# Set-up of a hybrid GLA and attention step: the first modulation vectors in two halves of the features

## The chip, the cores and the metric

One core of one Trainium2 chip. The metric is device time of one execution in microseconds (us): the median of three runs. Engines are named TensorE (PE in the rows, PEld its weight loads), VectorE (DVE), ScalarE (ACT), GpSimd (POOL) and SyncE (SP, which issues most DMAs).

## What is computed

Two layers over 256 context and 1024 latent tokens of width 1024. Only the first step of the first layer matters here: both token groups are normalised and modulated by vectors from a conditioning vector, and the result is projected.

```python
mod_p = (jax.nn.silu(c_ctx) @ w_ada[l] + b_ada[l])[None, None, :]
mod_s = (jax.nn.silu(c) @ w_ada[l] + b_ada[l])[:, None, :]
sh_s, sc_s, gt_s = split_mod(mod_s)
hs = rms_norm(xs, norm_g[l]) * (1.0 + sc_s) + sh_s
...
proj = h @ w_in
q, k, v, gate = jnp.split(proj, [GLA_QD, 2 * GLA_QD, 2 * GLA_QD + GLA_VD], axis=-1)
...
z = ((h @ wa1[d]) @ wa2[d] + ba[d]).astype(jnp.float32)
```

`w_ada[0]` is 1024 x 3072; shift and scale of layer 0 are its first 2048 columns, 8 MB in f32.

## The kernel before, in words

The hidden state `h` lies transposed in SBUF as two f16 tensors, `hT_hi` and `hT_lo` (high and low part), 8 tiles of 128 features by 1280 tokens. Each weight is split in the same way into `whi` and `wlo`, after scaling by a power of two; a product is three f16 matmuls (high by high, low by high, high by low). `pow2` finds such a power: a maximum for each partition on VectorE, one TensorE matmul that brings it across partitions into bank `o`, and some five one-column VectorE instructions (L87 to L102). Tokens come in three groups and chunks: the first 512 latent ones (group and chunk 0), the second 512, the 256 context ones.

The set-up (in `emit`) goes in this order:
- SyncE issues loads of the four token tiles `x` of group 0 (512 KB each), of two weight stages `wst` (1 MB each: queries and keys of the first heads), and of `w_ada` in eight row blocks of 1 MB, 8 KB for each partition, which land in places that are empty so early: `whi` and `wlo` of weight tiles 1 and 2, then `hT_hi` and `hT_lo`. Small constants, the next stage and the tokens of groups 2 and 1 (`ys`) follow; the low-rank decay weights come by GpSimd's queue.
- `cond_vectors`: the conditioning rows are transposed, SiLU is formed, and `cst` holds it as matmul weights. `normalise`: squares on ScalarE, mean-square step `nt_r4a` (L118), power -1/2 on GpSimd, then the rows `x` are scaled on VectorE (L352). TensorE transposes them, VectorE copies them to `xT` (L1327).
- `fill` makes `whi` on ScalarE (L190) and `wlo` on VectorE (L191) for the two stages; `split_rank` does the same for the low-rank decay weights.
- `mod_rows` sums all 2048 modulation values in 32 matmuls in bank `A` (L268), four of 512 columns side by side; the sums are copied, transposed in bank `cs` (L277) and get their bias (`modT`).
- `affine` forms gain and shift and their common power of two; its maximum is `af_m`, whose inverse is `inv_h`. `modulate` makes `h` on ScalarE (L370), `hT_hi` on GpSimd or ScalarE and `hT_lo` on VectorE, eight tiles of features one after another.
- `qk_pair` multiplies chunk 0 with the queries and keys of head 0: 48 matmuls of 512 columns (L495) in two `mm` banks over the 8 feature tiles. `rank` (low-rank decay, chunk 0) follows, then `ys` is normalised, transposed and modulated, and `qk_pair` runs for chunk 1, and so on.

Instructions are put in order by a scheduler for each engine (`issue_after` names one that must stand ahead), and each engine works through its rows in that order.

## Time and profile before

| | us |
|---|---|
| median of 3 runs | 1306.46 |
| lowest, highest | 1306.09, 1312.27 |
| the profiled execution: its own time | 1307.08 |
| the profiled execution: span of the core | 1305.20 |
| mean granted TensorE clock | 0.984 |

The span is from the first to the last instruction of the profile. Times in the rows are counted from its start; the rows come from that one execution.

### The profile page before, as it was taken

The numbers are of one execution on the slowest core, as the hardware profiler recorded it, in microseconds if no ns is written. First come the engines' busy times: TensorE is split into PE (matmuls) and PEld (weight loads), VectorE is DVE, ScalarE is ACT, GpSimd is POOL, SyncE is SP. The second block draws the span as 40 slices with busy tenths as digits, with TensorE's granted clock in tenths as the row PEclk, the third lists the DMA queues.
The fourth block names the chain that finished last, engine by engine and source line by source line (L and its number), as shares of the span: only waits on it lengthen the run. The fifth ranks groups of instructions, "written<-read, shape, count | busy, mean of one in ns | idle before, by whom it ended". The sixth has DMA issues, their size and how long they took to land. (4 is left out here: it accounts for less than half of the span.)

```text
span 1305.2 us, 22423 instructions
## 1 busy us (share of the span) xinstructions
PE 1222.4 (94%) x8015; PEld 791.3 (61%) x8015; DVE 907.5 (70%) x2110; ACT 713.3 (55%) x1730; POOL 370.9 (28%) x625
## 2 busy tenths in 40 slices
PE   4899999999998998798999889999999999989998
PEld 2366666555655556566877466667666666766444
DVE  5585879777876798666664667777667577786652
ACT  3684656565655566542443566666766677673110
POOL 1132214323322244311332643342233344322000
PEclk8899999999999999899999999999999999999999
DMA  9602745554646344257643376666947747879342
GB/s 366 245 33 82 219 149 179 168 158 130 189 139 195 116 150 142 82 150 261 162 120 108 91 179 130 126 131 133 202 105 167 141 87 145 175 151 236 126 153 81
DMA packets 335792, 199.12 MB, mean 153 GB/s; under 512 B 229838, under 2 KB 320446, under 8 KB 333376
## 3 DMA queue, kind: packets, MB, share of 16 engines
q1 hardware_dynamic: 328512, 180.79, 52.9%
q0 software_dynamic: 3728, 11.55, 2.7%
q10 hardware_dynamic: 3440, 5.35, 1.1%
q8 instruction: 63, 1.03, 0.3%
q14 instruction: 49, 0.40, 0.1%
HBM read 104.31 MB, written 37.24 MB: 108 GB/s over the span
## 5 line engine op out<-in xcount | busy, mean ns | idle before, releaser
L129 PEld LDWEIGHTS <-hT_hi 128*128 128x128 f16 x1920 | 188.7, 98 | 126.3 <-issue 12.8
L129 PE MATMUL mm<-whi,hT_hi 128*128 128x512 f16 (+1 forms) x576 | 200.6, 349 | 5.5 <-ACT gx L526 4.8
L129 PE MATMUL mm<-whi,hT_lo 128*128 128x512 f16 (+1 forms) x576 | 200.7, 348 | 0.0
L129 PE MATMUL mm<-wlo,hT_hi 128*128 128x512 f16 (+1 forms) x576 | 200.7, 348 | 0.0
L1094 DVE SCALAR_TENSOR_TENSOR phl<-p,srec,phl 128x1280 f16<-128x1280 f32 (+1 forms) x80 | 108.0, 1355 | 74.3 <-POOL phl L1091 43.5
L129 PEld LDWEIGHTS <-whi 128*128 128x128 f16 x1232 | 120.5, 98 | 61.6 <-issue 3.1
L129 PE MATMUL mm<-hT_hi,whi 128*128 128x256 f16 (+1 forms) x480 | 141.3, 294 | 0.7 <-ACT rope L1014 0.7
L129 PE MATMUL mm<-hT_lo,whi 128*128 128x256 f16 (+1 forms) x480 | 141.3, 294 | 0.0
L129 PE MATMUL mm<-hT_hi,wlo 128*128 128x256 f16 (+1 forms) x480 | 141.2, 294 | 0.0
L1061 PE MATMUL S<-kT,wst 128*128 128x512 f16 (+1 forms) x624 | 124.7, 342 | 11.5 <-ACT p L1069 11.5
L129 PEld LDWEIGHTS <-hT_lo 128*128 128x128 f16 x960 | 94.5, 98 | 61.6 <-issue 1.4
L129 PE MATMUL mm<-PT,vh 128*128 128x256 f16 x672 | 113.8, 275 | 8.8 <-DMA PT<-phl 6.0
L1091 POOL TENSOR_SCALAR phl<-p,srec 128x1280 f16<-128x1280 f32 (+1 forms) x40 | 55.4, 1384 | 200.4 <-DVE srec L1085 74.2
L1064 DVE TENSOR_REDUCE smx<-S 128x1 f32<-128x1280 f32 (+1 forms) x80 | 101.5, 1268 | 11.7 <-PE S L1061 11.7
L1069 ACT ACTIVATE p<-S,snb,sexp 128x1280 f32<-128x1280 f32 (+1 forms) x80 | 99.3, 1242 | 8.6 <-DVE phl L1094 3.7
L1061 PEld LDWEIGHTS <-wst 128*128 128x128 f16 x624 | 61.6, 99 | 66.1 <-issue 15.6
L129 PE MATMUL mm<-PT,vl 128*128 128x256 f16 x336 | 92.3, 275 | 0.0
L152 DVE TENSOR_REDUCE wmx<-wst 128x1 f32<-128x512 f32 x104 | 64.7, 676 | 22.0 <-DMA wst<-in_gla_w_in 8.7
L129 PEld LDWEIGHTS <-wlo 128*128 128x128 f16 x616 | 60.3, 98 | 31.5 <-DVE wlo L1222 1.8
L129 PEld LDWEIGHTS <-vh 128*128 128x128 f16 x672 | 65.6, 99 | 19.9 <-issue 8.3
L1066 ACT ACTIVATE snb<-smx,nsexp 128x1 f32<-128x1 f32 x80 | 23.3, 291 | 85.0 <-DVE smx L1064 84.8
L901 POOL TENSOR_TENSOR rope<-hx,ropet 128x64 f32<-128x64 f32 x160 | 63.1, 424 | 18.8 <-ACT hx L1027 11.2
(358 smaller groups left out, 2724.2 us busy)
## 6 DMA issues: line engine op xcount, KB each, us to landing
wada<-in_w_ada SPq DMA_DIRECT2D x16, 1024.0 KB
wst<-in_gla_w_in SPq DMA_DIRECT2D x12, 1024.0 KB
wst<-in_att_w_in SPq DMA_DIRECT2D x10, 1024.0 KB
og_d<-gx SPq DMA_DIRECT2D x40, 128.0 KB
og_d<-og POOLq DMA_DIRECT2D x40, 128.0 KB, 2.8
wst<-og_d SPq DMA_DIRECT2D x5, 1024.0 KB
xr<-x_d SPq DMA_DIRECT2D x9, 512.0 KB
out<-xr ACTq DMA_DIRECT2D x17, 256.0 KB
```

The source lines that it names most:

```text
L129: self.nc.tensor.matmul(out, a, b, start=k == 0 and j == 0, stop=k == n - 1 and j == 2)
L152: nc.vector.tensor_reduce(mx[:, j : j + 1], st[:, 2 * j : 2 * j + 2, :], AX.XY, ALU.max, apply_absolute_value=True)
L901: nc.gpsimd.tensor_tensor(tv[:, h, :, w, :], xv[:, h, :, 1 - w, :], sn[:, :, w, :], ALU.mult)
L1061: nc.tensor.matmul(S[:, a : a + n], x, y, start=m == 0, stop=m == 2)
L1064: last = nc.vector.tensor_reduce(mx, S, AX.X, ALU.max).ins
L1066: nc.scalar.activation(nb, mx, AF.Copy, scale=self.nsexp)
L1069: nc.scalar.activation(p, S, AF.Exp, scale=self.sexp, bias=nb, accum_out=den)
L1091: nc.gpsimd.tensor_scalar(hi, p, r, 2.0 ** 14, ALU.mult, ALU.mult)
L1094: nc.vector.scalar_tensor_tensor(lo, p, r2, hi, ALU.mult, ALU.subtract)
```

## The change

The columns of `w_ada` are loaded in two halves: first shift and scale of features 0 to 511 in eight pieces of 0.5 MB (two runs of 2 KB for each partition), into `hT_hi` and `hT_lo`, then those of features 512 to 1023 into the weight tiles. `mod_half` sums each half in 16 matmuls, in bank `A` and then `kt`; odd and even row blocks go to separate parts and are added on VectorE. `affine_half` gives the first half a power of two from its own maximum; the second takes the larger of both. Feature tiles 0 to 3 are modulated by the first half, and `qk_pair` sums 24 matmuls over them; after the second half it sums the other 24 and adds (L546 of the changed kernel). `rescale` brings the first four feature tiles of chunk 0 to the common power, for `rank`. SiLU is formed ahead of the mean-square step, two of four rows are normalised and four of eight `xT` copies made on ScalarE, and `split_rank` stands ahead of the two fills.

```diff
@@ -243,43 +243,85 @@
     def cond_vectors(self, rows, brow):
         nc, cp = self.nc, self.const
+        self.cst = self.t(cp, [P, KT, 32], F32, "cst")
+        nc.vector.memset(self.cst, 0.0)
         ps = self.bank("z")
         nc.tensor.transpose(ps[:, 0:32], rows, self.ident[0:32, 0:32])
-        nc.tensor.transpose(ps[:, 32:80], brow, self.ident[0:48, 0:48])
         cT = self.t(cp, [P, 80], F32, "cT")
-        nc.vector.tensor_copy(cT, ps[:, 0:80])
+        nc.vector.tensor_copy(cT[:, 0:32], ps[:, 0:32])
         self.gT = cT[:, 16:32]
         self.bT = cT[:, 32:80]
-        c = self.t(cp, [P, 16], F32, "silu_c")
-        nc.vector.tensor_copy(c, cT[:, 0:16])
+        c = cT[:, 0:16]
         self.silu(c, 16, "ls16")
-        self.cst = self.t(cp, [P, KT, 32], F32, "cst")
-        nc.vector.memset(self.cst, 0.0)
-        nc.vector.tensor_copy(self.cst[:, :, 0:2], c.rearrange("p (i k) -> p k i", i=2))
+        last = nc.vector.tensor_copy(self.cst[:, :, 0:2], c.rearrange("p (i k) -> p k i", i=2))
+        ps = self.bank("cs")
+        nc.tensor.transpose(ps[:, 0:48], brow, self.ident[0:48, 0:48])
+        nc.vector.tensor_copy(self.bT, ps[:, 0:48])
         self.modT = [self.t(cp, [P, 16, 2], F32, f"modT{l}") for l in range(2)]
-    def mod_rows(self, rows):
-        nc = self.nc
-        ps = self.bank("A")
+        return last.ins
+    def mod_half(self, u, rows):
+        nc = self.nc
+        ps = self.bank(("A", "kt")[u])
         for k, r in enumerate(rows):
-            for j in range(4):
-                nc.tensor.matmul(
-                    ps[32 * j : 32 * j + 32, :], self.cst[:, k, :], r[:, 512 * j : 512 * j + 512],
-                    start=k == 0, stop=k == KT - 1, tile_position=(0, 32 * j), skip_group_check=True,
-                )
+            with ExitStack() as c:
+                if k >= KT // 2:
+                    c.enter_context(self.tc.issue_after(self.cross))
+                for v in range(2):
+                    j = 2 * (k % 2) + v
+                    nc.tensor.matmul(
+                        ps[32 * j : 32 * j + 32, :], self.cst[:, k, :], r[:, v, :],
+                        start=k < 2, stop=k >= KT - 2, tile_position=(0, 32 * j), skip_group_check=True,
+                    )
         m = self.t(self.p1, [P, 512], F32, "mod")
         nc.scalar.copy(m[:, 0:256], ps[:, 0:256])
         nc.vector.tensor_copy(m[:, 256:512], ps[:, 256:512])
         ps = self.bank("cs")
         for b in range(4):
             nc.tensor.transpose(ps[:, b * P : b * P + P], m[:, b * P : b * P + P], self.ident)
-        nc.vector.tensor_tensor(
-            self.modT[0].rearrange("p (j b) i -> p j b i", j=4),
-            ps.rearrange("p (b j r) -> p j b r", b=4, j=4)[:, :, :, 0:2],
-            self.bT[:, 0:16].rearrange("p (j b) -> p j b", j=4).unsqueeze(3).to_broadcast([P, 4, 4, 2]), ALU.add,
-        )
+        part = ps.rearrange("p (b q v r) -> p q v b r", b=4, q=2, v=2)[:, :, :, :, 0:2]
+        to = self.modT[0].rearrange("p (v u b) i -> p u v b i", v=2, u=2)[:, u]
+        bias = self.bT[:, 0:16].rearrange("p (v u b) -> p u v b", v=2, u=2)[:, u].unsqueeze(3)
+        nc.vector.tensor_tensor(to, part[:, 0], bias.to_broadcast([P, 2, 4, 2]), ALU.add)
+        nc.vector.tensor_tensor(to, part[:, 1], to, ALU.add)
+    def affine_half(self, u):
+        nc, sp = self.nc, self.const
+        f = slice(4 * u, 4 * u + 4)
+        sh, sc = (self.modT[0][:, 8 * v : 8 * v + 8, :] for v in range(2))
+        if u == 0:
+            self.g0 = self.t(sp, [P, KT, 2], F32, "g0")
+            self.af = self.t(sp, [P, 2], F32, "af")
+        g = self.g0
+        gT = self.gT[:, f].unsqueeze(2).to_broadcast([P, 4, 2])
+        nc.vector.scalar_tensor_tensor(g[:, f], sc[:, f], 1.0, gT, ALU.add, ALU.mult)
+        m = self.t(self.small, [P, 2], F32, "wmx")
+        for j, t in enumerate((sh, g)):
+            nc.vector.tensor_reduce(m[:, j : j + 1], t[:, f], AX.XY, ALU.max, apply_absolute_value=True)
+        a = self.af[:, u : u + 1]
+        nc.vector.scalar_tensor_tensor(a, m[:, 1:2], 32.0, m[:, 0:1], ALU.mult, ALU.add)
+        if u == 1:
+            nc.vector.tensor_tensor(a, a, self.af[:, 0:1], ALU.max)
+        s, inv = self.pow2(a)
+        n = 4 + 4 * u
+        self.gs, self.sh = (self.t(sp, [P, n, 2], F32, f"{t}{n}") for t in ("gs", "sh"))
+        nc.vector.tensor_scalar(self.sh, sh[:, 0:n], s, None, ALU.mult)
+        nc.vector.tensor_scalar(self.gs, g[:, 0:n], s, None, ALU.mult)
+        if u == 1:
+            self.ratio = self.mulcol(s, self.inv_h, sp, "ratio")
+        self.inv_h = self.t(sp, [P, 1], F32, f"invh0{u}")
+        nc.vector.tensor_copy(self.inv_h, inv)
+    def rescale(self, c):
+        a, n = CHUNKS[c]
+        for t in (self.hT_hi, self.hT_lo):
+            x = t[:, 0 : KT // 2, a : a + n]
+            self.nc.vector.tensor_scalar(x, x, self.ratio, None, ALU.mult)
     def ada_load(self, l, b, to):
         self.nc.sync.dma_start(to, self.I["w_ada"][l, :, b * 256 : b * 256 + 256].rearrange("(k p) n -> p k n", p=P))
@@ -341,7 +383,7 @@
         return g, sh, c
-    def normalise(self, xs, junk):
+    def normalise(self, xs, junk, act=False):
         nc = self.nc
         n = len(xs)
         ssq = self.t(self.sm, [P, n], F32, f"nt_s{n}")
@@ -349,7 +391,10 @@
             nc.scalar.activation(junk, x, AF.Square, accum_out=ssq[:, j : j + 1])
         r = self.rstd(ssq, D, f"nt_r{n}")
         for j, x in enumerate(xs):
-            last = nc.vector.tensor_scalar(x, x, r[:, j : j + 1], None, ALU.mult)
+            if act and j % 2:
+                nc.scalar.activation(x, x, AF.Copy, scale=r[:, j : j + 1])
+            else:
+                last = nc.vector.tensor_scalar(x, x, r[:, j : j + 1], None, ALU.mult)
         return last.ins
     def transpose(self, xs, k, tag):
@@ -483,18 +528,26 @@
         self.qk[h][which][c] = out
-    def qk_pair(self, h, c, wq):
+    def qk_pair(self, h, c, wq, ks=range(KT), add=False):
         a, n = CHUNKS[c]
         banks = [self.bank("mm") for _ in range(2)]
-        for k in range(KT):
+        for k in ks:
             hh, hl = self.hT(k, a, n)
             for which, ps in enumerate(banks):
                 o = 256 * which + 128 * (h % 2)
                 wh, wl = (t[:, k, o : o + P] for t in wq[0:2])
                 for j, (x, y) in enumerate(((wh, hh), (wl, hh), (wh, hl))):
-                    self.nc.tensor.matmul(ps[:, :n], x, y, start=k == 0 and j == 0, stop=k == KT - 1 and j == 2)
+                    self.nc.tensor.matmul(
+                        ps[:, :n], x, y, start=k == ks[0] and j == 0, stop=k == ks[-1] and j == 2
+                    )
         for which, ps in enumerate(banks):
-            self.qk_out(h, which, c, ps[:, :n])
+            if add:
+                out = self.qk[h][which][c]
+                self.nc.vector.scalar_tensor_tensor(
+                    out, ps[:, :n], self.inv_qk[h // 2][which], out, ALU.mult, ALU.add
+                )
+            else:
+                self.qk_out(h, which, c, ps[:, :n])
     def tok_proj(self, i, w, ps):
         hi, lo = w[0:2]
@@ -1312,42 +1365,57 @@
             xs = group(0)
             wq = k.wtile(0)
             qk = [k.load_qk(wq, 0, j) for j in range(2)]
-            to = []
-            for t in (*k.wtile(1)[0:2], *k.wtile(2)[0:2], k.hT_hi, k.hT_hi, k.hT_lo, k.hT_lo):
-                a = 4096 * (len(to) % 2) if len(to) > 3 else 0
-                t = t.rearrange("p k n -> p (k n)")[:, a : a + 4096].bitcast(F32)
-                load(t, I["w_ada"][0, len(to) * P : len(to) * P + P, 0 : 2 * D])
-                to.append(t)
+            places = [t.rearrange("p k n -> p (k n)")[:, 2 * D * j : 2 * D * j + 2 * D]
+                      for t in (k.hT_hi, k.hT_lo, *k.wtile(1)[0:2], *k.wtile(2)[0:2])
+                      for j in range(4 if t is k.hT_hi or t is k.hT_lo else 2)]
+            to = [[], []]
+            for u in range(2):
+                for kk in range(KT):
+                    t = places.pop(0).bitcast(F32).rearrange("p (v n) -> p v n", v=2)
+                    ap = I["w_ada"][0, kk * P : kk * P + P, 0 : 2 * D]
+                    load(t, ap.rearrange("p (v u n) -> p u v n", v=2, u=2)[:, u])
+                    to[u].append(t)
             w = k.gla_consts()
-            k.cond_vectors(rows, brow)
+            cst = k.cond_vectors(rows, brow)
             junk = k.t(k.p1, [P, D], F16, "junk")
-            last = k.normalise(xs, junk)
+            with tc.issue_after(cst):
+                last = k.normalise(xs, junk, True)
             xT = k.t(k.p1, [P, KT, 512], F32, "xT")
             for kk in range(KT):
-                nc.vector.tensor_copy(xT[:, kk, :], k.transpose(xs, kk, ("z", "mm")[kk % 2]))
+                ps = k.transpose(xs, kk, ("z", "mm")[kk % 2])
+                if kk % 2:
+                    nc.scalar.copy(xT[:, kk, :], ps)
+                else:
+                    nc.vector.tensor_copy(xT[:, kk, :], ps)
             with tc.issue_after(last):
+                k.split_rank(*w)
                 run(qk[0])
                 run(qk[1])
-                cross = k.cross
-                k.split_rank(*w)
+            k.mod_half(0, to[0])
+            k.affine_half(0)
+            for kk in range(KT // 2):
+                act, dve = k.modulate(xT[:, kk, :], kk, GROUPS[0][0], kk % 2 == 1)
+            k.fold_qk(0, wq)
+            k.qk_pair(0, 0, wq, range(KT // 2))
             k.gla_tables()
             ys = group(1)
             wv = k.wtile(1)
             vf = k.load_v(wv, 0)
-            with tc.issue_after(cross), tc.issue_after(k.cross):
-                k.mod_rows(to)
+            k.mod_half(1, to[1])
             late = [t.rearrange("p k n -> p (k n)").bitcast(F32) for t in k.wtile(2)[0:2]]
             zs = [late[0][:, D * j : D * j + D] for j in range(2)]
             for j, x in enumerate(zs):
                 load(x, xrow(I, GROUPS[2][0] + j))
-            k.gs, k.sh, k.inv_h = k.affine(0)
-            for kk in range(KT):
+            k.affine_half(1)
+            for kk in range(KT // 2, KT):
                 act, dve = k.modulate(xT[:, kk, :], kk, GROUPS[0][0], kk % 2 == 1)
             k.fold_qk(0, wq)
             with tc.issue_after(act.ins), tc.issue_after(dve.ins):
                 k.rank_scales()
                 k.normalise(ys, junk)
-            k.qk_pair(0, 0, wq)
+            k.qk_pair(0, 0, wq, range(KT // 2, KT), True)
+            with tc.issue_after(dve.ins):
+                k.rescale(0)
             nxt = k.rank(0)
             for kk in range(KT):
                 act, dve = k.modulate(k.transpose(ys, kk, banks[kk % 6]), kk, GROUPS[1][0], kk % 2 == 1)
```

TensorE, from the last w_ada sums to the first chunk's matmuls, before. `A` is the bank of the sums, `cs` their transposes, `af_m` the cross-partition maximum, `mm` the queries and keys.

```order
L268 MATMUL A_330<-hT_hi_71,cst_166 32x512 x8
L268 MATMUL A_330<-hT_lo_72,cst_166 32x512 x8
L277 MATMUL cs_366<-ident_79,mod_363 128x128 x4
L87 LDWEIGHTS af_m_382
L87 MATMUL o_384<-ident_79,af_m_382 128x128
L495 LDWEIGHTS whi_16_120
L495 MATMUL mm_465<-hT_hi_71,whi_16_120 128x512
```

The same place in the changed kernel: `A` takes the first half's sums, `kt` the second's, in pieces of four or two matmuls.

```order
L275 MATMUL A_322<-hT_lo_72,cst_160 32x512 x4
L275 MATMUL kt_440<-whi_20_126,cst_160 32x512 x2
L284 MATMUL cs_342<-ident_79,mod_339 128x128 x2
L275 MATMUL kt_440<-whi_20_126,cst_160 32x512 x2
L284 MATMUL cs_342<-ident_79,mod_339 128x128 x2
L275 MATMUL kt_440<-wlo_21_127,cst_160 32x512 x4
L87 LDWEIGHTS af_350
L87 MATMUL o_356<-ident_79,af_350 128x128
L275 MATMUL kt_440<-whi_22_128,cst_160 32x512 x4
L275 MATMUL kt_440<-wlo_23_129,cst_160 32x512 x2
L540 LDWEIGHTS whi_16_120
L540 MATMUL mm_394<-hT_hi_71,whi_16_120 128x512
```

Four pieces of the second half now stand ahead of the first half's cross-partition matmul, and seven ahead of its first `mm` matmul; the eighth stands behind the tenth of these.

TensorE in the changed kernel, where the first half of the queries and keys ends and the second begins:

```order
L540 MATMUL mm_395<-hT_lo_72,whi_16_120 128x512
L284 MATMUL cs_460<-ident_79,mod_457 128x128 x4
L87 LDWEIGHTS af_350
L87 MATMUL o_477<-ident_79,af_350 128x128
L540 LDWEIGHTS whi_16_120
L540 MATMUL mm_546<-hT_hi_71,whi_16_120 128x512
```

The transposes of the second half's sums stand behind the last matmul of the first half, and nothing but the cross-partition matmul stands between them and the second half's matmuls.

VectorE ahead of the cross-partition maximum, before: the last fill of the decay weights, then the sums.

```order
L422 SCALAR_TENSOR_TENSOR wa_25_139<-wada_149,p2s_301,wa_25_139 34x1024
L274 COPY mod_363<-A_330 128x256
L278 TENSOR_TENSOR modT_38_169<-cs_366,cT_155 128x32
L329 SCALAR_TENSOR_TENSOR gs_91_376<-modT_38_169,cT_155 128x16
L333 TENSOR_REDUCE wmx_379<-modT_38_169 128x1
L333 TENSOR_REDUCE wmx_379<-gs_91_376 128x1
L335 SCALAR_TENSOR_TENSOR af_m_382<-wmx_379 128x1
L92 TENSOR_REDUCE p2m_386<-o_384 128x1
```

The same place in the changed kernel (`af` is the first half's maximum):

```order
L281 COPY mod_339<-A_322 128x256
L100 TENSOR_SCALAR p2s_310<-p2e_308 128x1
L102 TENSOR_SCALAR p2i_312<-p2e_308 128x1
L288 TENSOR_TENSOR modT_38_177<-cs_342,cT_164 128x2x8
L289 TENSOR_TENSOR modT_38_177<-cs_342,modT_38_177 128x2x8
L191 SCALAR_TENSOR_TENSOR wlo_17_121<-wst_124,p2s_310,whi_16_120 128x2x256
L301 SCALAR_TENSOR_TENSOR g_82_349<-modT_38_177,cT_164 128x8
L304 TENSOR_REDUCE wmx_352<-modT_38_177 128x1
L191 SCALAR_TENSOR_TENSOR wlo_17_121<-wst_124,p2s_310,whi_16_120 128x2x256
L304 TENSOR_REDUCE wmx_352<-g_82_349 128x1
L191 SCALAR_TENSOR_TENSOR wlo_17_121<-wst_124,p2s_310,whi_16_120 128x2x256
L306 SCALAR_TENSOR_TENSOR af_350<-wmx_352 128x1
```

The fills of the second weight stage (`wst_124`) now stand between the steps of the maximum: seven of the eight fills ahead of `af`, the eighth between it and the reduction of its cross-partition matmul.

## Rows read from the trace of the kernel before

**Rows 1.** Busy time by stretch: us and (instructions) by engine, granted clock, DMA share, GB/s.
```profile
0.00:65.00 65.00, 41.10 (x218) 18.78 (x219) 37.39 (x99) 32.45 (x53) 8.58 (x17) 0.89 0.84 307
65.00:400.00 335.00, 324.02 (x2048) 200.09 (x2046) 257.86 (x681) 199.89 (x504) 95.96 (x164) 0.99 0.47 146
```

**Rows 2.** Timeline, second group: start, duration, engine, line, operation; idle before and its releaser.
```profile
50.91 1.05 ACT L349 ACTIVATE junk<-x 128x1024 f16<-128x1024 f32 x1
...
55.62 0.17 DVE L118 TENSOR_SCALAR nt_r4a<-nt_s 128x4 f32<-128x4 f32 x1 [2.30 <-ACT junk L349]
56.93 2.74 DVE L352 TENSOR_SCALAR x<-x,nt_r 128x1024 f32<-128x1024 f32 x4 [1.13 <-POOL nt_r L120]
...
57.12 0.38 PE L495 MATMUL mm<-hT_lo,whi 128*128 128x512 f16 x1
...
61.57 0.78 ACT L370 ACTIVATE h<-z,sh,gs 128x512 f32<-128x512 f32 x1 [0.43 <-PE z L358]
...
63.56 0.38 PE L495 MATMUL mm<-hT_hi,whi 128*128 128x512 f16 x1
```

**Rows 3.** Timeline, from the first group's mean square to the first projection.
```profile
12.15 0.17 DVE L118 TENSOR_SCALAR nt_r4a<-nt_s 128x4 f32<-128x4 f32 x1 [10.99 <-ACT junk L349]
...
13.55 2.74 DVE L352 TENSOR_SCALAR x<-x,nt_r 128x1024 f32<-128x1024 f32 x4 [1.23 <-DMA wst<-in_gla_w_in]
...
35.67 1.29 DVE L422 SCALAR_TENSOR_TENSOR wa<-wada,p2s,wa 34x1024 f16<-34x1024 f32 x1
...
39.55 0.90 PE L277 MATMUL cs<-ident,mod 128*128 128x128 f32 x4 [0.49 <-ACT mod L273]
...
41.12 0.16 DVE L335 SCALAR_TENSOR_TENSOR af_m<-wmx 128x1 f32<-128x1 f32 x1
...
42.90 2.22 ACT L370 ACTIVATE h<-xT,sh,gs 128x512 f32<-128x512 f32 x3 [3.40 <-DVE gs L338]
...
44.48 0.58 PE L495 MATMUL mm<-hT_hi,whi 128*128 128x512 f16 x1 [2.91 <-POOL hT_hi L374]
```

**Rows 4.** Timeline: DMA issues behind the w_ada loads, and TensorE's wait for the last.
```profile
19.53 0.34 SPq L401 DMA_DIRECT2D sum<-in_k_sum  x1
...
26.98 0.38 SPq L404 DMA_DIRECT2D onorm<-in_gla_onorm  x1
...
37.99 0.16 PEld L268 LDWEIGHTS A<-hT_lo,cst 128*32 128x32 f32 x8 [0.90 <-DMA hT_lo<-in_w_ada]
```

**Rows 5.** DMA packets of three stretches: 20 to 30, 39 to 45, 45 to 54 us.
```profile
DMA packets 578, 4.21 MB, mean 421 GB/s; under 512 B 64, under 2 KB 64, under 8 KB 64
...
DMA packets 942, 2.38 MB, mean 397 GB/s; under 512 B 64, under 2 KB 464, under 8 KB 941
...
DMA packets 2352, 3.22 MB, mean 358 GB/s; under 512 B 77, under 2 KB 2061, under 8 KB 2352
```

**Rows 6.** VectorE from 12 to 37 us by line: count, busy us, mean ns, idle.
```profile
L191 DVE SCALAR_TENSOR_TENSOR wlo<-wst,p2s,whi 128x512 f16<-128x512 f32 x8 | 5.6, 742 | 0.0
...
L1327 DVE COPY xT<-z 128x512 f32<-128x512 f32 x4 | 2.7, 687 | 0.2 <-PE z L358 0.2
L352 DVE TENSOR_SCALAR x<-x,nt_r 128x1024 f32<-128x1024 f32 x4 | 2.7, 748 | 1.2 <-DMA wst<-in_gla_w_in 1.2
L1327 DVE COPY xT<-mm 128x512 f32<-128x512 f32 x4 | 2.6, 680 | 0.0
```

**Rows 7.** Timeline: the first ScalarE and the first VectorE step of SiLU.
```profile
22.57 0.21 ACT L230 ACTIVATE ls<-silu_c 128x16 f32<-128x16 f32 x1 [10.45 <-DVE silu_c L254]
...
25.96 0.17 DVE L233 SCALAR_TENSOR_TENSOR ls<-silu_c,ls 128x16 f32<-128x16 f32 x1
```

**Rows 8.** Busy time by stretch around the first projection, columns as in rows 1.
```profile
42.00:44.00 2.00, 0.00 (x0) 0.00 (x0) 1.19 (x9) 1.10 (x2) 0.19 (x1) 0.69 1.03 412
44.40:49.50 5.10, 5.02 (x12) 1.72 (x12) 3.38 (x5) 5.07 (x9) 1.56 (x4) 0.50 1.04 391
49.50:57.20 7.70, 7.70 (x37) 3.44 (x35) 3.90 (x14) 6.27 (x12) 1.34 (x2) 1.00 0.63 201
```

## The prediction

> **What bounds the kernel now.** I read the busy time by stretch first [rows 1]: up to 65 us TensorE works 41.1 of 65 us, from 65 to 400 us 324 of 335. So after the set-up the kernel is a TensorE queue that hardly waits, and the order of every engine behind the first chunks is the same rows in both programs (the listings differ only up to the transposes of the second group). What the change is worth is therefore one number: how far the first matmul of the second chunk's queries and keys moves, at 63.56 us now [rows 2]. I let that shift reach the end unchanged, since TensorE's waits behind it are on other engines of the same chain.
>
> What holds that matmul now, read backwards in the timeline [rows 2, 3]: the w_ada rows land until TensorE's wait at 37.99 us ends [rows 4]; sum, transposes, maximum, cross-partition matmul and modulation take until the first matmul at 44.48 us; 48 matmuls run to 57.5 us. Beside them ScalarE modulates until 50.91 us, then takes the squares of the second group (to 55.6 us), VectorE scales those rows from 56.93 to 59.67 us, and transposes and modulation follow.
>
> **DMA.** Half of the w_ada bytes are there at about 27 us: each issue behind the eight loads waits for one landing, the one at 26.98 us for the fourth [rows 4]. Pieces become runs of 2 KB instead of 8 KB. Neither is in the trace; runs of 8 KB moved at 421 GB/s, of 4 KB (mostly) at 397, of 1 KB (mostly) at 358 [rows 5]. I take 387, between the last two: 1.35 us for each 0.52 MB piece, so from 17.0 us (27 less four megabyte loads of 2.5 us) the first half is there at 27.9, the fourth piece of the second half at 33.3, the seventh at 37.3 and the last at 38.7. At 358 the last is there at 40.4, at 421 at 37.0. The bytes are no longer the first thing waited for; the engines are.
>
> **VectorE in front of the first sum.** The order listing puts nearly all fills of the query and key weights ahead of the first half's maximum `af`. Before, VectorE worked from 13.55 us to 36.96 us (the row at 35.67 plus 1.29) [rows 3], 23.4 us with hardly a gap. Of this go: four `xT` copies to ScalarE (2.6), two of the four normalising rows (1.4) [rows 6], small copies and SiLU steps moved ahead (0.6) and one fill, now behind the maximum (0.7). New in front: the bank copy, two additions, the gain, two reductions and the maximum, 1.3 by the 0.16 to 0.42 us of such instructions, and 0.4 waiting for the transposes: 19.8 us. The start is later, because SiLU now stands ahead of the mean-square step of 12.15 us: four ScalarE and three VectorE steps of some 0.2 us each [rows 7], 1.7 us, so 15.2. `af` is at about 35.2, where it was 41.12. From `af` to the first matmul it was 3.36 us [rows 3]; 0.3 more for the last fill in between. The first half's matmuls start at **38.9 us instead of 44.48**. TensorE's order puts seven of the second half's eight pieces ahead of them, but these are done by about 37.8, just in time: that cover is 1 us.
>
> **First half.** 24 matmuls. Now, the engine stood from about 40.5 to 44.48 us but for one small matmul; the granted clock fell (0.69 over 42 to 44 us), was 0.50 (1.2 GHz) for the 5.1 us from 44.40 (12 matmuls, 0.43 us each) and full (2.4 GHz) after 49.50 (0.21 us) [rows 8]. In the new order TensorE is again in small pieces ahead of 38.9. I take the same price: 10 matmuls at 0.43, the last two w_ada matmuls of 0.5, the rest at 0.21: 7.9 us, to 46.8. At full clock it would be 5.6.
>
> **Between the halves.** This is what the new order adds: the transposes of the second half's sums stand behind the last of those 24 matmuls, and everything that follows needs them. The same chain, from transposes at 39.55 to matmul at 44.48, is 4.93 us now [rows 3]; one more addition and one more maximum add 0.3. TensorE has nothing else in its queue meanwhile. Second half: 46.8 + 5.2 = **52.0 us**. So the clock falls and is paid a second time: 12 matmuls at 0.43 and 12 at 0.21, 7.7 us, to **59.7 us instead of 57.5**. The Trainium skill, in TensorE: Matmul & The Clock Gate, section HAM oscillation — how this bites in real kernels, speaks against such a cut: matmul bursts with waits between them pay the slow clock for every burst instead of once, and all of the contraction should be done before the next wait. By that rule the price above is paid twice, as I sum it; before shows it for one burst only.
>
> **The second group.** ScalarE's first modulation comes 1.6 us ahead of the matmul [rows 3]; eight took 8.0 us (42.90 to 50.91), four take 4.0: squares from 52.0 - 1.6 + 4.0 = 54.4, not 50.91. They last 4.7 us, to 59.1. VectorE's next step in that chain stands behind the addition of the second half's queries: 59.7 + 0.2 + 0.7 = 60.6 (at 55.62 now). Then as now: 1.31 us to the scaling, 2.74 us for four rows, 64.6. Now TensorE is still busy when they are done (the first modulation follows at 61.57, 1.9 us behind the last row); in the new order TensorE waits for them, so 0.35 us, and 1.99 us from the modulation to the matmul: 67.0. The rescaling is two f16 instructions of 2048 elements, between 0.75 us (one f32 row of 1024) and 1.5 us each; it lies beside the second half's matmuls, and without that cover would delay `rank` by up to 3 us, of which the wait for the second group hides most. Loads of the second group stand earlier in the queue and are there by about 46 us, ahead of the squares.
>
> Sum: 67.0 - 63.56 = **+3.4 us**. On the profiled execution (span 1305.2, time 1307.08) it is 1310.5; that execution is 0.6 above the median of the runs, so 1306.46 + 3.4 = **1309.9 us**. 0.5%, about what a measurement of this kernel can tell from no change, is 6.5 us.
>
> **Rivals.**
> - *The clock is paid once or not at all.* For it: the w_ada matmuls run until 1 us before the first half. Against: the fall between 40.5 and 44.48 after just such a stretch. Full in the first half: 2.2 less at 46.8 and all behind, +1.2, 1307.7. Full in the second: squares then set the end, 1.4 less, +2.0, 1308.5. Full in both: -0.2, 1306.3.
> - *VectorE or the loads are later.* The new small instructions and the waits between ScalarE's and VectorE's fills may cost 2 us more, or loads at 358 GB/s hold the seventh piece to 39.0 us: +0.7 to +2, 1310.6 to 1311.9.
> - *Slower: TensorE never reaches the upper clock in either half.* With 0.43 us throughout, 24 matmuls and the two w_ada ones take 10.8 us (2.9 more) and the second 24 take 10.3 (2.6 more): +8.9, 1315.4. For it: each half is only a little longer than the 5.1 us that the low clock lasted. Against: it did rise after them. It decides from 15 further matmuls at 0.43 on; 3.1 us more than I sum is past 6.5.
> - *Faster, as one reads the diff: the first sums come with the bytes at 28 us.* `af` at about 30 us, the first half at 33.5 and done before the second's bytes end; the second half then starts some 5 us behind the last piece, at about 44.5 at the earliest, so 7.5 less than above and about -5 at the end, 1301.5; by over 0.5% only if the clock is full too. Against: 19.8 us of VectorE work stand in front in its order.
>
> **How the numbers follow.** Clock paid twice 0.45; once 0.23; not at all 0.12; later engines or loads 0.08; low clock throughout 0.08; first sums with the bytes 0.04. The first four lie within 1306.3 and 1311.9. With 1.8 us for the scatter of the runs and the uncertain VectorE sum below, and 1.1 above, the range is 1304.5 to 1313.0; it leaves out the last two cases. Faster by over 0.5% 0.04 (the last case), slower by over 0.5% 0.08 (the low clock throughout), within 0.5% 0.88.
>
> **What would show it.** Right: the first `mm` matmul near 39 us and the 25th near 52, TensorE idle some 5 us between with VectorE's small chain in it, granted clock 0.5 at the start of both, squares from 54 us, the second chunk's first matmul near 67, and the same spacing behind it. Wrong: `af` on VectorE near 30 (its sum is off), a full clock at either start, the last w_ada piece behind 44 us (2 KB runs are slow), or a shift at 65 us that is not there at the end.

## The result, and the profile after

The changed kernel took 1310.26 us (median of 20 runs, 1305.86 to 1320.71), the kernel before 1306.70 us beside it (20 runs, 1300.07 to 1312.27): 3.6 us more by the medians, a ratio of 1.0036 with an interval of 1.0023 to 1.0048 (4.7 us, 3.0 to 6.3, of 1306.7). That is inside the half per cent that the prediction called no change, and 0.4 us from its number. The steps under it came out less well, as the profile shows. For the set-ups run alone, below, medians are given over all runs and over those within 1.5% of the fastest run of the same kernel.

Busy time by stretch of the changed kernel, columns as in [rows 1]:

```profile
0.00:65.00 65.00, 40.28 (x217) 17.79 (x218) 38.90 (x116) 35.93 (x58) 8.33 (x16) 0.97 0.88 306
65.00:400.00 335.00, 324.09 (x2052) 200.00 (x2051) 258.62 (x683) 201.29 (x506) 95.16 (x164) 0.99 0.47 146
```

TensorE's share ahead of 65 us and behind it is that of before; the granted clock of the first stretch is 0.97 where it was 0.89.

The timeline of the set-up after (start, duration, engine, line, operation, idle time before and its releaser). It answers to [rows 2, 3]:

```profile
11.56 1.06 ACT L391 ACTIVATE junk<-x 128x1024 f16<-128x1024 f32 x1 [1.81 <-DMA x<-in_x_sample]
...
15.49 1.42 DVE L397 TENSOR_SCALAR x<-x,nt_r 128x1024 f32<-128x1024 f32 x2 [1.12 <-POOL nt_r L120]
...
36.28 0.15 DVE L306 SCALAR_TENSOR_TENSOR af<-wmx 128x1 f32<-128x1 f32 x1
...
38.34 1.05 PE L275 MATMUL kt<-wlo,cst 128*32 128x512 f32 x4 [0.31 <-DMA wlo<-in_w_ada]
...
39.88 0.38 PE L540 MATMUL mm<-hT_hi,whi 128*128 128x512 f16 x1 [0.48 <-POOL hT_hi L419]
...
46.14 0.60 PE L284 MATMUL cs<-ident,mod 128*128 128x128 f32 x4
...
48.00 0.23 PE L87 MATMUL o<-ident,af 128*128 128x128 bf16 x1 [1.26 <-DVE af L308]
...
51.14 0.58 PE L540 MATMUL mm<-hT_hi,whi 128*128 128x512 f16 x1 [2.90 <-POOL hT_hi L419]
...
57.83 0.75 DVE L546 SCALAR_TENSOR_TENSOR q<-mm,iqk,q 128x512 f32<-128x512 f32 x1 [0.63 <-PE mm L540]
...
58.49 0.16 DVE L118 TENSOR_SCALAR nt_r4a<-nt_s 128x4 f32<-128x4 f32 x1
...
64.94 0.38 PE L540 MATMUL mm<-hT_hi,whi 128*128 128x512 f16 x1
```

The first row is the square of the fourth token tile, which starts when that tile has landed. The first half starts at 39.88 us, behind a w_ada piece whose bytes held TensorE until 38.34. The transposes of the second half's sums (`cs`) come at 46.14, its first matmul at 51.14; the factors (`nt_r4a`) of the second group and the second chunk's first matmul (the last row) follow. That last row stood at 63.56 before [rows 2]: the set-up is 1.4 us longer in these two traces, not 3.4.

The clock, in the same columns, for the first half, the gap, and two pieces of the second half. It answers to [rows 8]:

```profile
39.80:46.10 6.30, 6.22 (x28) 2.45 (x28) 3.12 (x5) 2.93 (x6) 0.65 (x2) 1.00 0.95 339
46.10:51.10 5.00, 0.87 (x6) 0.47 (x5) 2.65 (x18) 2.79 (x5) 0.62 (x1) 0.97 1.07 355
51.10:54.20 3.10, 3.06 (x8) 1.11 (x8) 2.49 (x4) 3.07 (x5) 0.62 (x1) 0.50 1.09 354
54.20:57.80 3.60, 3.60 (x18) 1.49 (x16) 2.90 (x12) 3.50 (x7) 0.00 (x0) 0.99 0.74 283
```

The first half ran at 1.00 from its first matmul to its last. Only 8 matmuls of the second half ran in the stretch at 0.50.

SyncE's queue, which shows how fast the pieces land (each of these issues waited for a landing). It answers to [rows 4]:

```profile
19.34 1.77 SPq L1376 DMA_DIRECT2D whi<-in_w_ada  x2
...
30.19 0.48 SPq L446 DMA_DIRECT2D sum<-in_k_sum  x1
```

Eight issues lie between the two, 10.85 us: 1.36 us for a piece of 0.52 MB, 387 GB/s. The prediction took 1.35 us. Each piece landed about 1 us later than its sum has it: the seventh of the second half held TensorE until 38.34 us (37.3 in the prediction).

How the shift against the kernel before goes on behind the set-up, in us. I worked it out from the timelines of VectorE and ScalarE: the median, over all rows that stand in the same order in both kernels, of their start less their start before. The last three columns are experiments below.

```
stretch before   changed   again   overlap   8 steps   16 steps
  80 to  120       1.4      0.7     -1.0       3.6       3.6
 160 to  200       2.4      1.1     -0.8       4.9       3.6
 280 to  320       0.5     -0.2     -1.3       2.8       1.5
 360 to  400       0.4     -0.1      0.9       3.0       1.7
 400 to  440       0.9      0.3      1.2      -0.3       2.5
 680 to  720       1.1      0.7      1.5       2.3       1.8
 960 to 1000       1.7     -2.5      2.0       3.0      -0.8
1040 to 1080       3.9     -0.3      4.6       5.3       1.9
     end           5.9      1.1      5.0       8.6       3.7
```

Each column is one execution. Within a column the shift wanders by 4 to 9 us, with no stretch at which all lose, so one trace cannot place the few us behind the set-up; the medians must be asked. The executions differ as a whole too: that of the changed kernel took 1312.86 us, above its median, that of again 1308.05, below its own.

### The profile page after: what moved, and what is told of

Same layout as the page of the kernel before. It is cut to its first block, busy times and chain, and to the rows that moved or that the text cites. A ratio compares the mean times of both kernels' runs of the same rounds, so it can differ in the third digit from the quotient of the medians.

```text
span 1311.1 us, 22470 instructions
## 1 busy us (share of the span) xinstructions
PE 1227.1 (94%) x8020; PEld 791.8 (60%) x8020; DVE 910.7 (69%) x2128; ACT 718.8 (55%) x1737; POOL 371.3 (28%) x625
## 5 line engine op out<-in xcount | busy, mean ns | idle before, releaser
L1114 PE MATMUL S<-kT,wst 128*128 128x512 f16 (+1 forms) x624 | 126.0, 345 | 10.5 <-ACT p L1122 10.4
L954 POOL TENSOR_TENSOR rope<-hx,ropet 128x64 f32<-128x64 f32 x160 | 63.1, 425 | 19.8 <-ACT hx L1080 12.1
```

The costliest lines, as they stand in the source:

```text
L954: nc.gpsimd.tensor_tensor(tv[:, h, :, w, :], xv[:, h, :, 1 - w, :], sn[:, :, w, :], ALU.mult)
L1114: nc.tensor.matmul(S[:, a : a + n], x, y, start=m == 0, stop=m == 2)
```

## The experiments

My theory: the set-up sets the price, by the chain between the halves and the low clock, and what it loses arrives whole at the end. The rivals: the start of the first half sets it (VectorE or loads); the low clock alone sets it; what costs lies behind the set-up.

### The changed kernel again (again), and both set-ups alone (setup_before, setup_after, setup_before2)

The first is the changed kernel unaltered. The set-ups alone are both kernels cut off behind the second chunk's rank sums, with four query and key tiles stored and everything behind left out:

```diff
+            for which in range(2):
+                for c in range(2):
+                    o = O[1][0].rearrange("(a p) d -> a p d", p=P)[4 * which + 2 * c]
+                    load(o[:, 0:512], k.qk[0][which][c])
+            return
```

Expected of the first: 

> The changed kernel once more, unaltered, for a second profile. Theory A (the difference is made in the set-up, and what follows carries it): the second chunk's first matmul again near 64.9 us, 1.4 later than in the kernel before, and behind it a shift against the kernel before that wanders by some 2 us either way, not always to the later side. Theory B (the rest of the 3.6 us is made behind the set-up, always at the same places): the shift grows again to some 4 us by 1040 us and to 5.9 at the end. Time 1308 to 1312 by both.

Of the set-up before: 

> The kernel before, ended behind the set-up: it stops when the second chunk's queries, keys and decay rank are summed and stores four query and key tiles, everything later is left out. Both theories: the second chunk's first matmul at 63.6 us as in the whole kernel, a time near 90 us with a scatter well under 1 us. It is the base for the next run.

Of the changed set-up: 

> The changed kernel, ended at the same place, everything later left out. Theory A1 (the set-up makes 1.4 us, as in the profile, in every run): 1.2 to 1.6 us longer than the run of the kernel before that ends there. Theory A2 (in most runs the clock of the first half is low, as I had forecast, and the profile shows a lucky one): 3 to 4 us longer, with more scatter. Theory B as A1; the rest of the 3.6 us would then lie behind the set-up.

Of the set-up before a second time, on the chip of the last cuts: 

> The kernel before cut off behind the set-up once more (everything behind is left out), beside the other cuts on one chip: 85.1 us if the side edits' 0.8 us is theirs; 85.6 to 86.0 if it is the chip's.

Measured: again 1312.39 us (12 runs) beside 1307.78, ratio 1.0020 (1.0001 to 1.0039). The set-ups alone: 85.14 us before (84.49 to 86.41, a wider scatter than expected), 86.01 the second time (85.42 to 87.08), and 87.59 changed (85.48 to 88.45; five of eight runs at 87.5 to 88.5, three at 85.5 to 86.1). All set-ups that ran alone, with those below:

| set-up alone | chip | median of all runs, us | of those within 1.5% |
|---|---|---|---|
| before | 4 | 85.14 | 84.97 |
| before, second time | 7 | 86.01 | 85.75 |
| changed | 4 | 87.59 | 86.04 |
| setup_overlap | 0 | 85.09 | 85.09 |
| setup_warm | 0 | 87.00 | 86.80 |
| setup_silu | 0 | 86.98 | 86.52 |
| setup_side | 0 | 85.95 | 85.95 |
| setup_overlap1 | 7 | 84.64 | 84.63 |

So the changed set-up costs 1.6 to 2.5 us by the medians of all runs, and 0.3 to 1.1 us by the last column. One and the same set-up differs by 0.9 us between two chips, and the changed one was not run on the chip of the next four: differences of under 1 us between them show nothing, and the traces must tell the rest. What hangs least on the start of the loads is the time from the first half's first matmul to the second chunk's first: 25.06 us in the changed kernel.

The changed set-up alone, timeline of one of its five long runs:

```profile
12.33 1.06 ACT L391 ACTIVATE junk<-x 128x1024 f16<-128x1024 f32 x1 [1.78 <-DMA x<-in_x_sample]
...
16.26 1.42 DVE L397 TENSOR_SCALAR x<-x,nt_r 128x1024 f32<-128x1024 f32 x2 [1.12 <-POOL nt_r L120]
...
40.86 0.38 PE L540 MATMUL mm<-hT_hi,whi 128*128 128x512 f16 x1 [1.08 <-POOL hT_hi L419]
...
47.13 0.60 PE L284 MATMUL cs<-ident,mod 128*128 128x128 f32 x4
...
52.12 0.59 PE L540 MATMUL mm<-hT_hi,whi 128*128 128x512 f16 x1 [2.90 <-POOL hT_hi L419]
...
59.07 0.19 ACT L391 ACTIVATION_READ_ACCUMULATOR junk<-x 128x1 f32 x1
...
59.62 0.75 DVE L546 SCALAR_TENSOR_TENSOR q<-mm,iqk,q 128x512 f32<-128x512 f32 x1 [1.44 <-PE mm L540]
60.29 0.16 DVE L118 TENSOR_SCALAR nt_r4a<-nt_s 128x4 f32<-128x4 f32 x1
...
66.77 0.38 PE L540 MATMUL mm<-hT_hi,whi 128*128 128x512 f16 x1
```

and its second half by stretch, columns as above:

```profile
52.10:56.90 4.80, 4.78 (x12) 1.75 (x12) 4.20 (x10) 4.73 (x8) 0.62 (x1) 0.50 0.00 0
56.90:59.60 2.70, 2.70 (x14) 1.09 (x12) 1.19 (x7) 2.30 (x4) 0.00 (x0) 1.00 0.00 0
```

Two things differ from the profile of the whole kernel. The fourth token tile landed at 12.33 and not 11.56 us, and VectorE's scaling stands 3.93 us behind it in both (15.49 less 11.56, 16.26 less 12.33). From there to the first half it is mostly VectorE's work, so a late load arrives at the first matmul, 0.98 us there. And the low clock lasted for 12 matmuls and not 8, so the second half's queries are added (`q`) only at 59.62 and the factors behind them start at 60.29, 1.0 us behind the end of the squares (59.26); from the first matmul to the second chunk it is 25.91 us. That these two make the long runs is in part argued, as no short run of this set-up has a trace; the mean granted clock fits it (0.945 to 0.950 in the five long runs, 0.961 to 0.970 in the three short ones). In again it is 25.07 us:

```profile
39.23 0.38 PE L540 MATMUL mm<-hT_hi,whi 128*128 128x512 f16 x1
...
50.48 0.59 PE L540 MATMUL mm<-hT_hi,whi 128*128 128x512 f16 x1 [2.90 <-POOL hT_hi L419]
...
64.30 0.38 PE L540 MATMUL mm<-hT_hi,whi 128*128 128x512 f16 x1
```

The set-up before waits for the last bytes of w_ada instead, and its runs lie closer.

### Half of the first half behind the cross-partition step (setup_overlap)

```diff
-            k.qk_pair(0, 0, wq, range(KT // 2))
+            held = k.qk_pair(0, 0, wq, range(KT // 2), part=range(SPLIT))
...
             k.affine_half(1)
+            with tc.issue_after(k.cross):
+                k.qk_pair(0, 0, wq, range(KT // 2), part=range(SPLIT, KT // 2), banks=held)
...
```

(`qk_pair` gets the two arguments `part` and `banks`.)

Expected, with SPLIT = 2: 

> The changed kernel cut off behind the set-up (it ends once the rank sums of the second chunk are issued and stores four query and key tiles; everything behind is left out), with the last 12 of the first half's 24 matmuls put behind the second half's cross-partition matmul, so that the bias transposes of the second half and its cross-partition matmul come 12 matmuls (12 x 0.21 = 2.5 us) earlier. Order theory (the second half is late because its sums stand on TensorE behind the whole first half): second half's first matmul not at 50.5 to 52.1 us but no earlier than the 12 matmuls and the chain allow, 48 to 49.6; the squares, the normalising factors and the second chunk's first matmul each about 2.5 us earlier (62.3 to 64.3), time 85.0 to 85.5 us against 87.6 for the changed set-up uncut in this way, so as the set-up before (85.1). Transfer theory (the second half waits for the second half's bytes of w_ada): nothing moves, 87.6. Clock theory (the low clock in the second half is what costs): the 12 matmuls fill the gap, the second half runs at the full clock as well, 2.5 + 2.5 us less, 82.5 to 83.5.

Measured: 85.09 us (84.87 to 85.30), less than the changed set-up by 2.5 us over all runs and by 1.0 in the last column. Timeline of TensorE:

```profile
40.30 0.39 PE L543 MATMUL mm<-hT_hi,whi 128*128 128x512 f16 x1
...
44.09 0.90 PE L287 MATMUL cs<-ident,mod 128*128 128x128 f32 x4
...
50.67 0.39 PE L543 MATMUL mm<-hT_hi,whi 128*128 128x512 f16 x1 [1.60 <-ACT q L530]
...
64.16 0.38 PE L543 MATMUL mm<-hT_hi,whi 128*128 128x512 f16 x1
```

The transposes stand at 44.09 instead of 47.13, behind the last w_ada piece; the 12 matmuls fill most of the gap (1.6 us of waiting are left), and the clock stays at 1.00. The second half starts at 50.67, not at the 48 to 49.6 expected: its banks come free when ScalarE has read the first half's (`ACT q`), so from the first half's first matmul to the second half's it is 10.4 us where it was 11.3. To the second chunk's it is 23.86 us: 1.2 us less than in the changed kernel and in again (8 matmuls at the low clock), 2.1 less than in the changed set-up alone (12). So the order of TensorE's rows is what the second half waited for, as the order theory has it; the bytes of w_ada were not.

### The gap filled with spare matmuls (setup_warm)

```diff
+            with tc.issue_after(k.cross):
+                spare = k.bank("U")
+                for _ in range(13):
+                    fill = nc.tensor.matmul(spare, wq[0][:, 0, 0:P], k.hT_hi[:, 0, 256:768], start=True, stop=True)
...
-            k.qk_pair(0, 0, wq, range(KT // 2, KT), True)
+            with tc.issue_after(fill.ins):
+                k.qk_pair(0, 0, wq, range(KT // 2, KT), True)
```

Expected: 

> The changed kernel cut off behind the set-up as before (everything behind is left out), with 13 spare matmuls of 512 columns, whose sums nobody reads, between the second half's cross-partition matmul and its first real one, so that TensorE works through the gap of 2.9 us ahead of the second half. Clock theory (the second half is long because the gap ahead of it lowers the clock): the granted clock stays 1.00 from 48 to 58 us, the second half takes 5.6 us and not 6.7 to 9, and the set-up is 1.2 to 2.6 us shorter, 85.0 to 86.4. Chain theory (behind the second half's modulation the squares on ScalarE, the factors and the rescaling set the second chunk's start, not the second half's matmuls): the second half ends 1 to 2 us earlier, the second chunk's first matmul does not move, 87.3 to 87.6.

Measured: 87.00 us (85.72 to 87.12), 0.6 less than the changed set-up over all runs, 0.8 more in the last column, so no gain that can be told; second half by stretch, and the timeline:

```profile
52.10:57.50 5.40, 5.34 (x24) 2.31 (x24) 4.70 (x13) 5.31 (x10) 0.63 (x2) 1.00 0.00 0
```

```profile
52.16 0.38 PE L540 MATMUL mm<-hT_hi,whi 128*128 128x512 f16 x1
...
59.49 0.16 DVE L118 TENSOR_SCALAR nt_r4a<-nt_s 128x4 f32<-128x4 f32 x1
...
65.95 0.38 PE L540 MATMUL mm<-hT_hi,whi 128*128 128x512 f16 x1
```

This parts the two causes. The second half starts where it did (52.16 against 52.12) and runs 24 matmuls in 5.4 us at 1.00, 2.3 us faster, but the second chunk gains only 0.82 us (66.77 to 65.95): ScalarE's squares end at 59.30, and the factors start at 59.49, directly behind VectorE's additions and small steps. From the first half's first matmul (40.91) to the second chunk's it is 25.04 us, the same as in the changed kernel with its 8 slow matmuls. So the low clock costs 0.9 us where it lasts for 12 matmuls and next to nothing where it lasts for 8; it is the smaller part.

### The normalising not held behind SiLU (setup_silu)

```diff
-            with tc.issue_after(cst):
-                last = k.normalise(xs, junk, True)
+            last = k.normalise(xs, junk, True)
```

Expected: 

> The changed kernel cut off behind the set-up as before (everything behind is left out), without the order that holds the normalising behind the SiLU steps: the four rows are scaled as soon as their squares are summed. VectorE theory (the first half starts when VectorE has done its 20 us of work, which begins with the normalising factor): VectorE starts about 1.7 us earlier, the first half's first matmul moves from 39.2 to 40.9 towards the time at which the next-to-last piece of sums allows it, about 39.4, and the set-up is 0.5 to 1.5 us shorter, 86.1 to 87.1. Transfer theory (the start is set by the bytes of the first half): nothing moves, 87.6.

Measured: 86.98 us (86.11 to 89.84), 0.6 less than the changed set-up over all runs, 0.5 more in the last column. Timeline:

```profile
12.60 1.06 ACT L391 ACTIVATE junk<-x 128x1024 f16<-128x1024 f32 x1 [1.44 <-DMA x<-in_x_sample]
...
40.04 0.38 PE L540 MATMUL mm<-hT_hi,whi 128*128 128x512 f16 x1
...
41.91 1.05 PE L275 MATMUL kt<-wlo,cst 128*32 128x512 f32 x4 [0.85 <-DMA wlo<-in_w_ada]
...
51.79 0.59 PE L540 MATMUL mm<-hT_hi,whi 128*128 128x512 f16 x1 [2.90 <-POOL hT_hi L419]
...
60.19 0.74 DVE L546 SCALAR_TENSOR_TENSOR k<-mm,iqk,k 128x512 f32<-128x512 f32 x1
60.84 0.16 DVE L118 TENSOR_SCALAR nt_r4a<-nt_s 128x4 f32<-128x4 f32 x1
...
67.30 0.38 PE L540 MATMUL mm<-hT_hi,whi 128*128 128x512 f16 x1
```

The last token tile was later still (12.60), and yet the first half starts 0.82 us earlier than in the changed set-up, behind the piece of w_ada as forecast. TensorE then waits 0.85 us for the last piece (41.91), so an earlier start of VectorE soon meets the bytes, and the second half gains 0.33 us. But the factors now stand behind both additions (`k` at 60.19), and the second chunk is 0.5 us later in this trace. The gain at the start stands in one trace; the times show none.

### The side edits alone (setup_side)

```diff
-            k.cond_vectors(rows, brow)
+            cst = k.cond_vectors(rows, brow)
...
-            last = k.normalise(xs, junk)
+            with tc.issue_after(cst):
+                last = k.normalise(xs, junk, True)
...
+                if kk % 2:
+                    nc.scalar.copy(xT[:, kk, :], ps)
+                else:
+                    nc.vector.tensor_copy(xT[:, kk, :], ps)
```

Expected: 

> The kernel before cut off behind the set-up in the same way (everything behind is left out), with the change's side edits alone: SiLU ahead of the normalising, two of the four normalising rows and four of the eight transposed copies on ScalarE, the rank weight's split ahead of the first query weights'; w_ada is loaded and used in one piece as before. Transfer theory (before, the sums wait for the last of 8.4 MB of loads, and VectorE's work ahead of it is hidden): second chunk's first matmul at 63.4, time 85.1 as the set-up before, within 0.4. VectorE theory (the edits shorten what the start waits for): 0.5 to 1.5 us shorter, 83.6 to 84.6. If the side edits themselves are what cost the change its time, 87.

Measured: 85.95 us (85.60 to 86.27), between nothing and 0.8 more than the set-up before (85.14 and 86.01), so nothing that can be told from the chip. Its trace by stretch is instructive (the first row is the set-up before, the others this one):

```profile
34.00:38.00 4.00, 3.72 (x30) 0.92 (x30) 2.60 (x5) 1.60 (x2) 0.00 (x0) 1.00 1.03 346
```

```profile
34.00:38.00 4.00, 1.30 (x12) 0.16 (x8) 1.03 (x2) 0.00 (x0) 0.00 (x0) 0.89 1.03 370
38.00:44.00 6.00, 3.37 (x13) 0.91 (x14) 2.15 (x13) 0.37 (x1) 0.00 (x0) 0.50 1.02 398
```

VectorE is done earlier, so TensorE has less to do beside the sums (1.30 us busy of 34 to 38, 3.72 in the set-up before), and the clock falls ahead of the last sums: 0.50 from 38 us on.

### More of it behind (setup_overlap1), and the whole kernel (full_overlap)

With SPLIT = 1, 18 matmuls stand behind. Expected: 

> The changed kernel cut off behind the set-up as before (everything behind is left out), with 18 and not 12 of the first half's matmuls behind the second half's cross-partition matmul. Order theory alone would give a second half 1.3 us earlier than with 12, 49.4 us, and 83.8 us; but the second half's sums take the banks that the first half's sums leave, and those leave only behind its last matmul: with 18 still to run, the second half's first matmul stands at 50.5 or later, and the time is 84.9 to 85.5 as with 12. The next-to-last bytes of w_ada (sums at 42.6 us in the cut with 12) hold the order as well.

Measured: 84.64 us (84.04 to 85.70) beside 86.01 for the set-up before on that chip, 1.4 us less (1.1 in the last column): the only one of these differences that was taken on one chip with the set-up before. TensorE's rows:

```profile
45.97 0.63 PE L543 MATMUL mm<-hT_hi,whi 128*128 128x512 f16 x1
...
51.61 0.39 PE L543 MATMUL mm<-hT_hi,whi 128*128 128x512 f16 x1
```

The 18 follow at once (45.97), the first of them at the low clock, and the second half waits for them until 51.61, as the banks' account has it (the second chunk's first matmul stands at 64.57); the time lies a little below the range given.

The whole changed kernel with SPLIT = 2. Expected: 

> The whole changed kernel with the last 12 of the first half's 24 matmuls behind the second half's cross-partition matmul. The set-up was 2.5 us shorter by it when cut off there (85.09 against 87.59 us), as long as the set-up before (85.14). Carry theory (what the set-up loses is carried whole to the end): 0 us against the kernel before, 1306 to 1309, ratio 0.999 to 1.001, where the changed kernel had 1.0036 and 1.0020. Rival (what the change costs arises behind the set-up, or is a chance of the runs): 1310 to 1313, ratio 1.002 to 1.004.

Measured: 1312.06 us (1307.49 to 1318.52, 12 runs) beside 1308.35, ratio 1.0031 (1.0014 to 1.0049). In its trace the set-up is good:

```profile
49.10 0.39 PE L543 MATMUL mm<-hT_hi,whi 128*128 128x512 f16 x1 [1.60 <-ACT q L530]
...
62.59 0.38 PE L543 MATMUL mm<-hT_hi,whi 128*128 128x512 f16 x1
```

The second chunk starts at 62.59, 1.0 us ahead of before [rows 2] and 23.84 us behind the first half's first matmul, as in the cut, and the kernel is as slow as the changed one. This is against my theory: the set-up's loss was taken away, and the time did not come back. One thing else differs: rows of all engines but GpSimd that stand between 560 and 600 us come in another order than in the changed kernel, whose order there is that of before.

### A set-up made late on purpose (delay24, delay16)

```diff
+        for _ in range(8 if l == 0 else 0):
+            nc.vector.tensor_scalar(g, g, 1.0, None, ALU.mult)
```

Expected of the first (delay24): 

> The kernel before with 24 spare one-step multiplications by 1 on VectorE inside the affine step of layer 0, each waiting for the one before, between the factors and the scaled queries of the first chunk: nothing else changed. By 8 of the three-instruction chains of the same engine at 0.15 to 0.19 us from start to start, they hold the first matmul up by about 4 us. Carry theory: 4 us more at the end, 1311.5 to 1312.5, ratio about 1.003. Absorb theory (a later wait for a transfer takes up what the set-up loses): 0 to 1 us more, ratio 1.000 to 1.001.

The code that ran as delay24 had 8 such steps, as shown, not 24; it is read as 8 here. The second has 16. Expected of it: 

> The kernel before with 16 spare one-step multiplications by 1 on VectorE in the affine step of layer 0, each waiting for the one before (nothing else added). The run called delay24 turned out to carry 8 such steps and not 24: its trace shows them as 8 rows of 0.2 us from start to start, 1.8 us from the scaled factors to the first modulation, and its rows behind the set-up stand in another order than in the kernel before (as do those of full_overlap against the changed kernel); it was 5.2 us slower. With 16 the rows of VectorE, ScalarE and SyncE all stand as before, and those of TensorE all but six transposes of the second chunk. The first matmul comes 3.3 us later. Carry theory (each us of the set-up arrives at the end): 3.3 us slower, 1311 to 1312, ratio 1.002 to 1.003; then the other order is what cost the 8 steps and full_overlap some 3.5 us more. Absorb theory (a transfer that is waited for near 400 us takes the delay up, as the traces of the 8 steps, 3.0 us behind at 360 to 400 us and 0.3 ahead at 400 to 440, suggest): 0 to 1 us, ratio 1.000 to 1.001. Sensitive theory (any shift of the set-up costs later, by waits that fall otherwise): 5 us or more, ratio 1.004 or above.

Measured: 8 steps 1313.55 us (6 runs, 1312.78 to 1316.49) beside 1308.35, ratio 1.0055 (1.0040 to 1.0070); 16 steps 1311.79 us (12 runs) beside 1306.05, ratio 1.0041 (1.0020 to 1.0061). First matmul of the two, with 8 steps and with 16:

```profile
47.78 0.58 PE L497 MATMUL mm<-hT_hi,whi 128*128 128x512 f16 x1 [4.70 <-POOL hT_hi L376]
```

```profile
47.78 0.58 PE L497 MATMUL mm<-hT_hi,whi 128*128 128x512 f16 x1 [6.37 <-POOL hT_hi L376]
```

From the maximum to this matmul it is 5.15 us with 8 steps (maximum at 42.63) and 6.82 with 16 (at 40.96), where it was 3.36 [rows 3]: 1.8 and 3.5 us of delay. At the end the 16 steps cost 5.4 us (2.6 to 8.0, of 1306), which holds 3.5, but also the 5 us and more of the sensitive theory: between the two nothing is decided. The 8 steps, with later rows in another order, cost 7.2 (5.2 to 9.2), which does not hold 1.8. The absorb theory fails by the medians, though one place can take up a delay: TensorE waits near 392 us for a step of GpSimd. Waits of TensorE from 385 to 402 us, in all, times, longest, in the kernel before, with 16 and with 8 steps:

```profile
PE A L646 <- POOL at L592: 4.2, 1, 4.2
```

```profile
PE A L648 <- POOL at L594: 4.2, 1, 4.2
```

```profile
PE A L648 <- POOL at L594: 0.9, 1, 0.9
```

Where the wait shrank to 0.9, the shift went from 3.0 to -0.3 us, and came back later.

## Why the prediction was right, and which steps were not

**The time.** 1309.9 forecast, 1310.26 measured, +3.4 against +3.6 by the medians. The sum that gave +3.4 was for the set-up, which came out at +1.4: the first half started 1.0 us later than forecast, the first half itself took 1.6 less, the gap 0.2 less, the second half 1.2 less, and the rest was as summed. Some 2 us of the 3.6 arise elsewhere. That the number came out is therefore luck: two errors cancelled. One of the prediction's own signs of being wrong, a full clock at either start, came true. Three of its sums do not give what stands there: 15.2 and 19.8 us make 35.0, not 35.2, for `af`; the first half's terms make 8.2 us, not 7.9, and 6.0, not 5.6, at full clock; in the rival of the first sums with the bytes, 7.5 us earlier than a shift of +3.4 is -4.1, not -5. None of this moves the forecast by more than 0.3 us.

**DMA: the rate was right.** 1.36 us for a piece against 1.35, with every piece about 1 us late. The bytes were not what the second half waited for.

**VectorE in front of the first sum: nearly.** Scaling from 15.49 (15.2 forecast), `af` at 36.28 (35.2), so 20.8 us of work instead of 19.8; from `af` to the first matmul 3.60 (3.66). The first half starts at 39.88 (38.9). What I missed is that this start follows the landing of the fourth token tile: in the seven traces with this order of VectorE's rows the tile lands between 10.40 and 12.69 us, and the first matmul stands 27.9 to 28.5 us behind it. The seventh piece of w_ada ends near the same time, so in some of them (again at 39.23) TensorE comes straight from it.

**First half: the step that failed.** "I take the same price": it was not paid. TensorE worked on w_ada pieces until 39.4 us and stood for half a microsecond, where before it stood for 2.9 [rows 3]; the granted clock was 1.00, and the half, with the last piece inside, took 6.3 us and not 7.9. This is the rival in which the clock is paid once, full in the first half, which I gave +1.2 at the second chunk; the two whole traces show +1.4 and, again, +0.7.

**Between the halves: right.** From the transposes to the second half's first matmul 5.0 us (5.2 forecast), TensorE idle but for one small matmul. That this order costs the set-up time is shown by the overlap's traces, 1.2 us back against the changed kernel's; its median says 1.0 to 2.5, from another chip.

**Second half: right in kind.** The clock fell in the gap as forecast, for 8 to 12 matmuls; with 8 it is 6.7 us from the first matmul to the addition of the queries, where the sum has 7.9 with 12. That it weighs 0.9 us at most, and next to nothing with 8, is shown by the spare matmuls; behind a full clock the squares end 0.2 us ahead of the factors, so they set the end almost as the rival's arithmetic had it. The Trainium skill, TensorE: Matmul & The Clock Gate, section HAM oscillation — how this bites in real kernels, has bursts behind waits for data pay each time. In the trace the second, behind the gap, paid, and the first, with half a microsecond in front of it, did not, so the rule does not reach the first. The Trainium skill, TensorE: Matmul & The Clock Gate, section What's actually happening, reports 6, 11 or 14 slow matmuls for one and the same kernel; the 8 of the changed kernel, 8 of the same again and 12 of the cut agree with a count that varies.

**"I let that shift reach the end unchanged": not borne out.** The set-up costs 1.4 and 0.7 us in the two whole traces and 0.3 to 2.5 in the cuts; the whole kernel 4.7 (3.0 to 6.3) and, again, 2.6 (0.1 to 5.1). These can be reconciled, but the overlap can't: its set-up is as short as that of before, in the cut and in one whole trace, and the kernel 4.1 us slower (1.8 to 6.4). So some us arise behind the set-up in the overlap and with the 8 steps; in the changed kernel the medians suggest it, and with the 16 steps nothing asks for it. Whether the changed order of later rows does it (it is there in the overlap and the 8 steps, not in the changed kernel and the 16) or the way in which later waits fall when the set-up is shifted or rebuilt, stays open; no run isolates it. No version beat the kernel before: the shortest set-up, with 18 matmuls moved, was run only as a cut.

## What to carry to other kernels

Cutting a contraction in two so that the first part runs beside the loads leaves TensorE standing while the second part's scales are made, unless something else fills its queue: putting part of the first half behind the cross-partition step, not in front of it, made the set-up 1.2 to 2.1 us shorter in the traces here, though the whole kernel did not become faster. Work moved off the wait for bytes onto one engine's queue inherits that queue's start, here the landing of the last token tile. A gain or loss of 2 us in the set-up of a kernel of 1300 us can't be read from one profile, nor taken to its end without a measurement.

## What the runs showed of the hardware that was not expected

The granted clock was 1.00 from 28.0 to 39.8 us of the changed kernel, in which TensorE did mostly w_ada pieces, 9.0 us busy in all, with waits of 0.3 to 1.2 us between them. In the set-up with the side edits alone a stretch of 34 to 38 us with 1.30 us of work saw it falling (0.89, then 0.50). The low stretch behind the same gap held 8, 8 and 12 matmuls in three executions of the same rows. A rescaling of 2048 f16 elements on VectorE took 0.75 us, as long as one of 1024 f32 elements [rows 6].
